# Gated linear attention in a hybrid trunk: keeping the 32x32 diagonal blocks of the scores in a compact array and multiplying them into the output block by block

## The chip, the cores and the metric

The kernel runs on one core of one Trainium2 chip. The metric is the device time of one execution in microseconds (us). The kernel before takes 1256.16 us, the median of 3 runs (1253.02 to 1259.6).

## What is computed

The reference is one layer of a trunk in which one input projection feeds four head groups (RetNet retention, gated DeltaNet, an S5 state space and GLA, gated linear attention); their gated outputs are concatenated and projected back. The change lies in the GLA group: 4 heads, keys 32 wide, values 64 wide, 2048 positions.

```python
def _gla(q, k, v, gk):                      # 4 heads, dk = 32, dv = 64
    cum = cumsum(gk within a chunk)
    rel = where(causal, cum_i - cum_j, -inf)
    scores[i, j] = sum_d q[i, d] * k[j, d] * exp(rel[i, j, d])
    o_intra = scores @ v                    # within the chunk
    state   = state * exp(cum_last) + (k * exp(cum_last - cum)).T @ v
    o_inter = (q * exp(cum)) @ state_before # from earlier chunks
    return o_intra + o_inter

y_gla = head_rmsnorm(o) * silu(gate)
out   = x + rmsnorm(concat(y_ret, y_dn, y_s5, y_gla) @ w_out)
```

## The kernel before, in words

All stages run on the one core, one after another, with neighbours overlapping: retention together with the S5 input projection, then GLA (`phase_gla`, L1198) with the S5 scan woven in as `side` steps, then DeltaNet (`phase_dn`), then the output projection (`phase_out`).

`phase_gla` works on 16 tiles of 128 positions, and a tile is treated as one chunk. For tile i the loop at L1387 issues `decays(i + 1)` (cumulative gate, its differences, exponentials; tile `gE`), `scores(i, 0)` for heads 0 and 1, the first half of the dense projections of later tiles (f16 products at L301 and L309 into `pa`), `output(i - 1)`, `mid(i)` (which loads and rescales the weights of DeltaNet after tiles 8, 9, 11 and 12; the rescaling on VectorE is L265), `scores(i, 1)` for heads 2 and 3, and the second half of the dense work. The S5 steps (lines 869 to 992; tiles `s5U`, `s5T`, `s5st`, `z`) run between the dense products. Small steps are put off with `later` and `string`, which release a chain of operations a few dense products apart, and with `due`, which issues what a buffer's next user needs. All operations so recorded carry line L153, so they are told apart by their tiles. The framework sets the final order of each engine's instructions from priorities and a timing model of its own; each engine then works through its list in order.

The scores of a tile are transposed (keys on partitions, queries along the row) and come in two kinds. The parts off the diagonal 32x32 blocks come out of PSUM straight into `gsT` ([128, 4, 128], one per tile parity) by three ScalarE copies (`copies`, L1337 to L1339). The diagonal 32x32 blocks are made of six levels, each a 32x32 product per block (L1299, 48 for two heads); `fin` (L1318) masks and adds them on VectorE for two heads at a time: one masked product `gpm` (128x384), one addition `gs` of 128x192 (tag `gs1`), one of 128x64 (tag `gs2`), and then four additions of 32x64, one for each 32-partition strip, that write the block to its place on the diagonal of `gsT` (L1330 to L1332). So `fin` is 7 VectorE operations for two heads, 14 a tile.

`output(i)` (L1347) takes the bank `o` (one buffer), multiplies the carried state (`gSbd`, L1351), adds the four heads' `gsT` times `gv` (L1353: 128x128 by 128x64 in f32), transposes `kl` (L1357), and later updates the state (L1363, L1367). `finish` squares, normalises and gates the result (`fsq`, `fss`, `fry`, `frt`, `frr`).

Elsewhere in the kernel small f32 products share a bank as the new ones do: in `dn_back` of DeltaNet (L1778 and L1779) the products alternate between the two 64-partition halves, and both halves of `pu` lie in one PSUM bank, as do both of `pw`.

Of the kernel before, what the change touches and what calls it, by code (L numbers as in the profile page):

```python
# [11 lines left out]
ALU = mybir.AluOpType  # L12
# [143 lines left out]
class Trunk:  # L156
# [1041 lines left out]
    def phase_gla(self, last, then, mid, side):  # L1198
        nc, A, NT = self.nc, self.A, self.NT
        NU = NT // 2  # L1200
        wqk, dqk = self.W["gqk"]
        P = self.pool("gla", bufs=2, side="right")
# [6 lines left out]
        nc.gpsimd.memset(Sbd, 0.0)  # L1209
        St = [S, Sbd]  # L1210
        blk = self.c("glablk")
        q2, k2, gk2, v, g, qk, q7, kl, el, done = ({} for _ in range(10))

        def stream(out, ops, fin):

# [75 lines left out]
        def scores(i, hp):  # L1291
            tk = slice((i % 2) * 128, (i % 2) * 128 + 128)
            q, k = q2[i // 2][:, tk], k2[i // 2][:, tk]
            sT = sT2[i % 2]
            box = []

            def mm(e, po, pn, c0, lh, rh, col):
                r = slice(32 * (2 * hp + e), 32 * (2 * hp + e) + 32)
                nc.tensor.matmul(box[0][po:po + pn, e, c0:c0 + rh.shape[1]], lh[r], rh[r], start=True, stop=True, tile_position=(32 * (2 * hp + e), col))  # L1299

            def first():
                self.due(lambda r, at: r == "gE")
                box.extend((self.ps("sc2"), self.count["sc2"]))

            yield first
            for e in range(2):
                yield lambda e=e: mm(e, 0, 64, 192, qk[i][:, 0, 0:64], qk[i][:, 0, 64:128], 0)
            for o, c0 in ((64, 64), (96, 0)):
                for e in range(2):
                    yield lambda e=e, o=o, c0=c0: mm(e, o, 32, 192, qk[i][:, 1, c0:c0 + 32], qk[i][:, 1, c0 + 32:c0 + 64], o)  # L1310
            for lv in range(6):
                for B in range(4):
                    cb = slice(32 * B, 32 * B + 32)
                    lh, rh = (qk[i][:, 2 + lv, cb], qk[i][:, 2 + lv, cb]) if lv < 5 else (k[:, cb], q[:, cb])
                    for e in range(2):
                        yield lambda e=e, B=B, lv=lv, lh=lh, rh=rh: mm(e, 32 * B, 32, lv * 32, lh, rh, 32 * B)

            def fin():  # L1318
                sc = box[0]
                ops = []  # L1320
                V = Later(nc.vector, ops)
                pm = self.t(P, [128, 2, 6, 32], "gpm")
                V.tensor_tensor(pm.rearrange("p e l i -> p e (l i)"), sc[:, :, 0:192],
                                msk.unsqueeze(1).to_broadcast([128, 2, 192]), op=ALU.mult)
                s1 = self.t(P, [128, 2, 3, 32], "gs1")
                V.tensor_tensor(s1, pm[:, :, 0:3, :], pm[:, :, 3:6, :], op=ALU.add)
                s2 = self.t(P, [128, 2, 32], "gs2")
                V.tensor_tensor(s2, s1[:, :, 0, :], s1[:, :, 1, :], op=ALU.add)
                sv = sT[:, 2 * hp:2 * hp + 2, :]
                for B in range(4):  # L1330
                    cb = slice(32 * B, 32 * B + 32)
                    V.tensor_tensor(sv[cb, :, cb], s2[cb], s1[cb, :, 2, :], op=ALU.add)  # L1332
                self.string(0, 3, ops, "sc2", box[1])

            def copies():
                sc, sv = box[0], sT[:, 2 * hp:2 * hp + 2, :]
                nc.scalar.activation(sv[0:64, :, 64:128], sc[0:64, :, 192:256], AF.Copy)  # L1337
                nc.scalar.activation(sv[64:96, :, 96:128], sc[64:96, :, 192:224], AF.Copy)
                nc.scalar.activation(sv[0:32, :, 32:64], sc[96:128, :, 192:224], AF.Copy)  # L1339

            def parts():
                done[i] = box[1]
                self.later(2, copies, "sc2", box[1])
                self.later(6, fin, "sc2", box[1])
            yield parts

        def output(i):  # L1347
            self.due(lambda r, at: r == "sc2" and at <= done[i])
            bank = self.ps("o")
            po, pk, pS = bank[:, 0:256], bank[:, 256:384], bank[:, 384:448]  # L1350
            nc.tensor.matmul(po, q7[i], St[1].rearrange("p h d -> p (h d)"), start=True, stop=False)  # L1351
            for h in range(4):
                nc.tensor.matmul(po[:, h * 64:(h + 1) * 64], sT2[i % 2][:, h, :], v[i][:, h, :], start=False, stop=(h == 3))  # L1353
            at = self.count["o"]
            if i + 1 < NT:
                kT = self.t(P, [128, 128], "gkT")
                nc.tensor.transpose(pk, kl[i], self.c("ident"))  # L1357
                nc.scalar.activation(kT, pk, AF.Copy)

                def update():  # L1360
                    for h in range(4):
                        r = slice(32 * h, 32 * h + 32)
                        nc.tensor.matmul(pS[r], kT[:, r], v[i][:, h, :], start=True, stop=True, tile_position=(0, 32 * h))  # L1363

                def state():
                    S = self.t(P, [128, 64], "gS")
                    nc.vector.scalar_tensor_tensor(S, St[0], el[i], pS, op0=ALU.mult, op1=ALU.add)  # L1367
                    Sbd = self.t(P, [128, 4, 64], "gSbd")
                    nc.gpsimd.tensor_tensor(Sbd, S.unsqueeze(1).to_broadcast([128, 4, 64]), blk.unsqueeze(2).to_broadcast([128, 4, 64]), op=ALU.mult)
                    St[:] = [S, Sbd]  # L1370

                self.later(10, update, "o", at)
                self.later(18, state, "o", at)
            self.finish(P, po, lambda: g[i], self.half(self.W["gg"][1], 4.0), 3, i)
# [5 lines left out]
        sT2 = [self.t(P1, [128, 4, 128], f"gsT{i}") for i in range(2)]  # L1380
# [6 lines left out]
        for i in range(NT):  # L1387
            self.due(lambda r, at: r == "gE")
            if i + 1 < NT:
                decays(i + 1)  # L1390
            dense = [v_ops(i + 1)] if i + 1 < NT else []
            dense += [g_ops(i)]
            u, part = (i + 3) // 2, (i + 1) % 2
            if u < NU:
                dense.insert(2 - part, qk_ops(u, part))
            dense = list(chain(*dense))
            h = len(dense) // 2

            for op in scores(i, 0):
                op()  # L1400
            self.emit(dense[:h], [side] * 2)
            if i > 0:
                output(i - 1)
            mid(i)
            for op in scores(i, 1):
                op()
            self.emit(dense[h:], [side])
        output(NT - 1)
        self.gP1, self.gP = P1, P

# [563 lines left out]
```

## Time and profile before

| what | value |
|---|---|
| median of 3 runs | 1256.16 us (1253.02 to 1259.6) |
| the profiled execution | 1256.04 us |
| span of its trace | 1253.8 us |
| mean granted TensorE clock | 0.937 of full speed |
| TensorE busy | 1129.3 us (90%) |
| VectorE busy | 960.0 us (77%) |
| ScalarE busy | 481.5 us (38%) |
| GpSimd busy | 459.8 us (37%) |

The profiled execution lies 0.1 us under the median of the runs, and 2.2 us of it lie outside the span. The shares are means over the whole kernel. The stage of the change is the loop over tiles in `phase_gla`; its first score product starts 327 us into the span and its last output product ends at 601 us, so the questions to ask of the trace are which engine is busy there, and what TensorE waits for there. In the rows PE is TensorE, DVE is VectorE, ACT is ScalarE and POOL is GpSimd.

### The profile page before, as it was taken

The numbers are of one execution on the slowest core, as the hardware profiler recorded it, in microseconds if no ns is written. First come the engines' busy times: TensorE is split into PE (matmuls) and PEld (weight loads), VectorE is DVE, ScalarE is ACT, GpSimd is POOL, SyncE is SP. The second block draws the span as 40 slices with busy tenths as digits, with TensorE's granted clock in tenths as the row PEclk, the third lists the DMA queues.
The fourth block names the chain that finished last, engine by engine and source line by source line (L and its number), as shares of the span: only waits on it lengthen the run. The fifth ranks groups of instructions, "written<-read, shape, count | busy, mean of one in ns | idle before, by whom it ended". The sixth has DMA issues, their size and how long they took to land. (4 is left out here: it accounts for less than half of the span.)

```text
span 1253.8 us, 37473 instructions
## 1 busy us (share of the span) xinstructions
PE 1129.3 (90%) x15175; PEld 933.1 (74%) x15175; DVE 960.0 (77%) x3429; ACT 481.5 (38%) x1076; POOL 459.8 (37%) x848
## 2 busy tenths in 40 slices
PE   4889999999899998988789989898899999899997
PEld 2767888888787777766667667676777777788886
DVE  7779655346899999998787676887888745778786
ACT  6623322126344444452433223342343453434332
POOL 3112121102755555552533423433423213434342
PEclk8899999999899999888989779898999989999999
DMA  8565611101211112121212112112112625566653
GB/s 291 142 159 137 166 64 68 35 22 60 62 30 35 35 35 55 35 55 22 86 45 33 27 21 38 26 51 39 29 50 44 157 80 149 180 182 177 190 132 104
DMA packets 186908, 104.91 MB, mean 84 GB/s; under 512 B 158000, under 2 KB 173552, under 8 KB 184560
## 3 DMA queue, kind: packets, MB, share of 16 engines
q1 hardware_dynamic: 186160, 102.00, 31.5%
q8 instruction: 119, 1.95, 0.6%
q10 hardware_dynamic: 576, 0.52, 0.1%
q14 instruction: 53, 0.43, 0.1%
HBM read 59.43 MB, written 26.23 MB: 68 GB/s over the span
## 5 line engine op out<-in xcount | busy, mean ns | idle before, releaser
L301 PEld LDWEIGHTS <-xT 128*128 128x128 f16 x3456 | 340.2, 101 | 82.4 <-issue 21.5
L301 PE MATMUL pa<-w,xT 128*128 128x256 f16 x3072 | 390.2, 283 | 6.7 <-DVE w L265 3.3
L309 PE MATMUL pa<-xT,w 128*128 128x256 f16 x1536 | 213.6, 290 | 14.4 <-ACT raw L1465 11.2
L309 PEld LDWEIGHTS <-w 128*128 128x128 f16 x1536 | 151.5, 103 | 44.1 <-issue 15.5
L1850 PE MATMUL o<-w,yT 128*128 128x256 f16 x1344 | 153.9, 275 | 6.7 <-DMA yT<-y 6.4
L1850 PEld LDWEIGHTS <-yT 128*128 128x128 f16 x1344 | 131.5, 98 | 26.6 <-DMA yT<-y 9.3
L153 DVE SCALAR_TENSOR_TENSOR cva<-raw,cw,cva 128x256 f32<-128x256 f32 x144 | 79.5, 554 | 1.4
L1861 POOL TENSOR_TENSOR ot<-of,npost 128x256 f32<-128x256 f32 x64 | 56.7, 904 | 47.4 <-ACT of L1859 47.2
L153 ACT ACTIVATE gE<-gE 128x384 f32<-128x384 f32 x96 | 43.8, 513 | 76.7 <-DVE gE L153 34.3
L265 DVE SCALAR_TENSOR_TENSOR w<-stg,wgs,w 128x256 f16<-128x256 f32 x96 | 52.4, 602 | 10.9 <-POOL w L262 10.0
L301 PE MATMUL pa<-wsu,xT 128*128 128x280 f16 x384 | 52.9, 298 | 8.2 <-DVE rgg L375 3.6
L1464 POOL COPY raw<-raw 128x3 f32<-128x3 f32 x48 | 14.8, 315 | 108.6 <-DVE cva L153 54.8
L1147 POOL TENSOR_TENSOR ropq<-ropm,ropn 128x256 f32<-128x256 f32 x16 | 12.8, 797 | 110.3 <-DVE ropn L1144 102.4
L371 ACT ACTIVATE th<-pa,hd 128x256 f32<-128x256 f32 x64 | 30.1, 470 | 53.8 <-PE pa L301 51.7
L408 ACT ACTIVATE fsq<-o 128x256 f32<-128x256 f32 x48 | 18.2, 379 | 82.1 <-PE o L1195 56.3
L153 DVE TENSOR_TENSOR gsT<-gs,gs 32x64 f32<-32x64 f32 x128 | 46.0, 360 | 1.9
L1860 DVE SCALAR_TENSOR_TENSOR ojk<-of 128x256 f32<-128x256 f32 x64 | 40.2, 629 | 9.4 <-ACT of L1859 6.8
L1285 POOL TENSOR_TENSOR gE<-gE,gk 128x64 f32<-128x64 f32 x112 | 34.3, 337 | 30.2 <-ACT gE L153 21.8
L1796 POOL TENSOR_TENSOR dKG<-dkh,dkgd 64x256 f32<-64x256 f32 x32 | 23.1, 721 | 57.8 <-PE c L1810 50.3
L153 DVE TENSOR_REDUCE fss<-fsq 128x4 f32<-128x256 f32 x48 | 19.8, 413 | 30.7 <-ACT fsq L408 30.6
L1476 ACT ACTIVATE cvt<-cva 128x256 f32<-128x256 f32 x48 | 19.9, 415 | 60.6 <-DVE cva L153 32.5
L1299 PE MATMUL sc<-gE 32*32 32x32 f32 (+1 forms) x2944 | 40.3, 203 | 2.5 <-DVE KK L910 2.5
(418 smaller groups left out, 2313.0 us busy)
## 6 DMA issues: line engine op xcount, KB each, us to landing
x<-in_x SPq DMA_DIRECT2D x16, 512.0 KB, 4.5
stg<-in_wi SPq DMA_DIRECT2D x8, 1024.0 KB, 4.8
yo<-y_d SPq DMA_DIRECT2D x14, 512.0 KB, 4.6
xo<-in_x SPq DMA_DIRECT2D x14, 512.0 KB, 3.6
out<-xo SPq DMA_DIRECT2D x13, 512.0 KB, 3.7
y_d<-fsq SPq DMA_DIRECT2D x48, 128.0 KB, 1.9
xT<-in_wi SPq DMA_DIRECT2D x4, 1024.0 KB, 7.0
rope<-in_rope SPq DMA_DIRECT2D x16, 256.0 KB, 3.2
```

Source lines behind the costliest of these rows:

```text
L153: return lambda *a, **k: self.ops.append(lambda: getattr(self.engine, name)(*a, **k))
L265: nc.vector.scalar_tensor_tensor(dst[:, 1, k, :], st[:, k, :], gs[:, k:k + 1], dst[:, 0, k, :], op0=ALU.mult, op1=ALU.subtract)
L301: yield lambda k=k, i=i, a=a, b=b: self.nc.tensor.matmul(out, xt[:, a, k, t0:t0 + 128], w[:, b, k, :], start=(k == 0 and i == 0), stop=(k ...
L309: yield lambda k=k, i=i, a=a, b=b: self.nc.tensor.matmul(out, w[:, b, k, c0:c0 + 128], xt[:, a, k, :], start=(k == 0 and i == 0), stop=(k ...
L371: nc.scalar.activation(th, ps[0], AF.Tanh, scale=self.half(dsc))
L1285: eng.tensor_tensor(x, x, src.rearrange("p (n w) -> p n w", w=2 * b)[:, :, a:a + b], op=ALU.mult)
L1299: nc.tensor.matmul(box[0][po:po + pn, e, c0:c0 + rh.shape[1]], lh[r], rh[r], start=True, stop=True, tile_position=(32 * (2 * hp + e), col))
L1476: nc.scalar.activation(th[0], a, AF.Tanh, scale=0.5)
L1796: nc.gpsimd.tensor_tensor(KG[r, c], f["kh"][r, t], f["kgd"][r, t, :].unsqueeze(2).to_broadcast([64, 4, 64]), op=ALU.mult)
L1850: nc.tensor.matmul(o, yT[:, a, k, :], w[:, b, k, :], start=(k == 0 and q == 0 and j % per == 0), stop=(k == 7 and q == 2 and j % per == pe ...
L1860: nc.vector.scalar_tensor_tensor(jk, of[:, cs], 1.0, of[:, cs], op0=ALU.mult, op1=ALU.mult, accum_out=so[:, j:j + 1])
L1861: nc.gpsimd.tensor_tensor(t1[:, cs], of[:, cs], npost[:, cs], op=ALU.mult)
```

## The change

`gpm`, `gs1` and `gs2` now hold all four heads of a tile. For heads 0 and 1 `fin` does only the masked product, into the first half of `gpm`. For heads 2 and 3 it does the masked product into the second half and then three additions for all four heads: 128x384 into `gs1`, 128x128 into `gs2`, and 128x128 in place in `gs2`. `fin` is 5 VectorE operations a tile, where it was 14. The diagonal blocks are no longer written to `gsT`, where they stay at the zeros of the start. `output` adds 16 products of 32x32 by 32x64 in f32, one for each head and each 32-partition strip, which take `gs2` straight and add to the same bank `o`.

```diff
@@ scores / fin @@
-                pm = self.t(P, [128, 2, 6, 32], "gpm")
-                V.tensor_tensor(pm.rearrange("p e l i -> p e (l i)"), sc[:, :, 0:192],
+                if hp == 0:
+                    pms[i] = self.t(P, [128, 4, 6, 32], "gpm")
+                pm = pms[i]
+                V.tensor_tensor(pm[:, 2 * hp:2 * hp + 2].rearrange("p e l i -> p e (l i)"), sc[:, :, 0:192],
                                 msk.unsqueeze(1).to_broadcast([128, 2, 192]), op=ALU.mult)
-                s1 = self.t(P, [128, 2, 3, 32], "gs1")
-                V.tensor_tensor(s1, pm[:, :, 0:3, :], pm[:, :, 3:6, :], op=ALU.add)
-                s2 = self.t(P, [128, 2, 32], "gs2")
-                V.tensor_tensor(s2, s1[:, :, 0, :], s1[:, :, 1, :], op=ALU.add)
-                sv = sT[:, 2 * hp:2 * hp + 2, :]
-                for B in range(4):
-                    cb = slice(32 * B, 32 * B + 32)
-                    V.tensor_tensor(sv[cb, :, cb], s2[cb], s1[cb, :, 2, :], op=ALU.add)
+                if hp == 1:
+                    pms.pop(i)
+                    s1 = self.t(P, [128, 4, 3, 32], "gs1", bufs=1)
+                    V.tensor_tensor(s1, pm[:, :, 0:3, :], pm[:, :, 3:6, :], op=ALU.add)
+                    s2 = self.t(P, [128, 4, 32], "gs2")
+                    sD[i] = s2
+                    V.tensor_tensor(s2, s1[:, :, 0, :], s1[:, :, 1, :], op=ALU.add)
+                    V.tensor_tensor(s2, s2, s1[:, :, 2, :], op=ALU.add)
                 self.string(0, 3, ops, "sc2", box[1])
@@ output @@
             for h in range(4):
-                nc.tensor.matmul(po[:, h * 64:(h + 1) * 64], sT2[i % 2][:, h, :], v[i][:, h, :], start=False, stop=(h == 3))
+                nc.tensor.matmul(po[:, h * 64:(h + 1) * 64], sT2[i % 2][:, h, :], v[i][:, h, :], start=False, stop=False)
+            D = sD.pop(i)
+            for h in range(4):
+                for o in range(0, 128, 32):
+                    r = slice(o, o + 32)
+                    nc.tensor.matmul(po[r, h * 64:(h + 1) * 64], D[r, h, :], v[i][r, h, :], start=False, stop=(h == 3), tile_position=(o, o))
```

## Rows read from the trace of the kernel before

**Rows 1.** stretches of the GLA loop: length, engines' busy time, clock, DMA

```profile
core 0: us, PE busy (x) PEld busy (x) DVE busy (x) ACT busy (x) POOL busy (x), PEclk, DMA share, GB/s
327.00:347.00 20.00, 16.03 (x378) 12.84 (x378) 18.50 (x40) 10.55 (x27) 19.25 (x41) 0.83 0.36 90
347.00:485.00 138.00, 128.96 (x2844) 108.44 (x2833) 132.87 (x442) 57.97 (x167) 79.63 (x197) 0.99 0.18 34
485.00:561.00 76.00, 67.49 (x1362) 54.51 (x1349) 71.38 (x242) 36.83 (x97) 44.83 (x100) 0.87 0.20 53
561.00:601.00 40.00, 34.15 (x665) 27.03 (x664) 31.90 (x122) 10.46 (x30) 11.18 (x27) 0.87 0.09 21
```

**Rows 2.** waits, 327 to 601 us, engine PE: total us, times, longest

```profile
PE z L932 <- ACT s5UT L920: 8.6, 5, 2.7
PE sc L909 <- DVE gpm L153: 4.0, 1, 4.0
PE o L1351 <- DVE fsq L153: 3.8, 3, 1.9
PE sc L982 <- DVE gpm L153: 3.2, 1, 3.2
```

**Rows 3.** groups by line, DVE, 327 to 601 us: busy us, mean ns, idle

```profile
L153 DVE TENSOR_TENSOR gsT<-gs,gs 32x64 f32<-32x64 f32 x128 | 46.0, 360 | 1.9
...
L153 DVE TENSOR_TENSOR gpm<-sc,glamask 128x384 f32<-128x384 f32 x32 | 17.4, 545 | 1.3 <-ACT gsT L1339 1.3
L153 DVE TENSOR_TENSOR gE<-gE 128x128 f32<-128x128 f32 x56 | 15.9, 291 | 0.0
...
L153 DVE TENSOR_TENSOR gs<-gpm 128x192 f32<-128x192 f32 x32 | 14.9, 466 | 0.5
...
L153 DVE TENSOR_TENSOR gs<-gs 128x64 f32<-128x64 f32 x32 | 8.9, 279 | 0.5
```

**Rows 4.** order of time (start us, length us), DVE, ACT, PE [idle before]

```profile
408.32 2.49 DVE L153 TENSOR_TENSOR gsT<-gs,gs 32x64 f32<-32x64 f32 x4
...
410.95 0.28 DVE L153 TENSOR_TENSOR gE<-gE 128x128 f32<-128x128 f32 x1
...
411.32 1.35 ACT L153 ACTIVATE gE<-gE 128x384 f32<-128x384 f32 x3 [2.31 <-DVE gE L153]
...
413.67 0.60 ACT L920 ACTIVATE s5UT<-z 128x512 f32<-128x512 f32 x1
...
414.32 1.08 PE L932 MATMUL z<-s5UT,s5PT 128*64 128x256 f32 x8 [2.66 <-ACT s5UT L920]
```

**Rows 5.** order of time, 541 to 549 us, DVE, then PE

```profile
541.33 5.32 DVE L265 SCALAR_TENSOR_TENSOR w<-stg,wgs,w 128x256 f16<-128x256 f32 x8 [0.47 <-POOL w L262]
...
546.89 1.57 PE L1299 MATMUL sc<-gE 32*64 32x64 f32 x88 [2.53 <-DVE KK L910]
```

**Rows 6.** order of time, PE: a tile's output, state update, next output

```profile
400.11 1.00 PE L1353 MATMUL o<-gv,gsT 128*128 128x64 f32 x8
...
404.29 0.32 PE L1363 MATMUL o<-gv,gkT 128*32 128x64 f32 x8
404.54 0.39 PE L309 MATMUL pa<-xT,w 128*128 128x256 f16 x2
...
417.63 1.00 PE L1353 MATMUL o<-gv,gsT 128*128 128x64 f32 x8
```

**Rows 7.** order of time, PE, 689 us: first and last of 58 instructions

```profile
689.11 0.22 PE L1779 MATMUL l<-dT,dkg 64*64 64x64 f32 x1
689.12 0.22 PE L1778 MATMUL l<-dv,dT 64*64 64x64 f32 x1
...
689.17 0.22 PE L1779 MATMUL l<-dT,dkg 64*64 64x64 f32 x1
...
689.94 0.22 PE L1779 MATMUL l<-dT,dkg 64*64 64x64 f32 x1
```

More of the change, by code (lines that the diff above doesn't have):

```diff
@@ L1211, in phase_gla @@
         blk = self.c("glablk")
-        q2, k2, gk2, v, g, qk, q7, kl, el, done = ({} for _ in range(10))
+        q2, k2, gk2, v, g, qk, q7, kl, el, done, pms, sD = ({} for _ in range(12))
         def stream(out, ops, fin):
```

## The prediction, made before the changed kernel ran

> **What bounds the kernel now.** I read the trace from the stage inwards: first the busy times of the GLA loop by stretch, then the waits of TensorE in it, then VectorE's groups by cost, then the order of time around single waits. The loop lasts 274 us, from 327 to 601, for 16 tiles: 17.1 us a tile. Adding up the four stretches, VectorE is busy 18.50 + 132.87 + 71.38 + 31.90 = 254.65 us (93%) and TensorE 246.63 us (90%) [rows 1]. Neither is at its full rate all the time: TensorE is idle 3.97, 9.04, 8.51 and 5.85 us in the four stretches, 27.4 us in all, and its granted clock is 0.83, 0.99, 0.87 and 0.87 there, which costs 0.17 x 20 + 0.01 x 138 + 0.13 x 76 + 0.13 x 40 = 19.9 us of full-speed work [rows 1]. So about 47 of the 274 us are not TensorE work at full speed, and some 227 us are. The reader should see that two engines are close to full at once: relieving VectorE can give back at most those 47 us, and whatever is added to TensorE is paid from them.
>
> Who makes TensorE wait? The longest sums are 8.6 us for `s5UT` from ScalarE, 4.0 and 3.2 us for the masked product `gpm` on VectorE, and 3.8 us for `fsq` on VectorE [rows 2]. The ScalarE wait is VectorE's too, as one case shows in order of time: the four strip additions hold VectorE for 2.49 us from 408.32; the difference `gE` queued behind them starts at 410.95; ScalarE's `gE`, which had idled 2.31 us for it, starts at 411.32; `s5UT`, next in ScalarE's list, starts at 413.67; and TensorE, idle 2.66 us, goes on at 414.32 [rows 4]. The very operations that the change removes stand at the head of that chain.
>
> **The change part by part.**
>
> **VectorE.** Removed are 128 strip additions (46.0 us), 32 additions of 128x192 (14.9) and 32 of 128x64 (8.9), together 69.8 us or 4.36 us a tile; the two masked products a tile stay [rows 3]. Added a tile are one addition of 128x384 and two of 128x128. The trace has no addition of 128x384 in this place: the masked product of that size takes 545 ns, and two of 128x192 would take 2 x 466 = 932 ns [rows 3]; I take 650, nearer to the row of the same size. For 128x128 the row is 291 ns [rows 3]; the second, in place and dependent on the first, I put at 330 (bounds 280 to 360, the last being the strip's own mean). Sum: 0.65 + 0.29 + 0.33 = 1.27 us a tile (bounds 1.11 to 1.65). Saved: 3.09 us a tile (2.7 to 3.25), 49 us in the loop. VectorE then has 254.65 - 49 = 205 us of work, and is no longer what fills the loop.
>
> **TensorE.** Added are 16 products a tile. The four products of L1353 stand in the trace as 8 instructions [rows 6], two for each product in f32, so the new ones are 32 instructions a tile; nothing is removed, since L1353 still multiplies whole 128x128 blocks. The nearest rows are small f32 products of the same 64 columns that fill different parts of the array: 58 instructions start between 689.11 and 689.94, 57 steps of 14.6 ns [rows 7]. Their blocks are 64x64 where the new ones are 32x32, but they too go four at a time to separate parts. That gives 32 x 14.6 = 0.47 us. Going to another block shape and back is not free: the 8 instructions of L1363 hold TensorE from 404.29 to 404.54, 0.25 us [rows 6], against 8 x 14.6 = 0.12, so I add 0.13. Together 0.60 us a tile, 9.6 us in the loop. Lower bound 0.47 (7.5 us); upper bound at L1363's own rate, 32 x 0.25 / 8 = 1.0 us (16 us).
>
> In the rows at 689 us, L1778 and L1779 start within 10 to 20 ns of one another though each lasts 220 ns, and both halves of `pu` lie in one bank [rows 7]: products from different rows of the array overlap while they write the same bank. The Trainium skill, page "TensorEngine Tiling (Array Packing)", section "Restrictions and Gotchas", says the opposite: "Different row tiles cannot access same PSUM bank simultaneously". The new products are just that, four row groups into the one bank `o`. By that sentence they would go singly, and the loop would lose instead of gain (the second rival has its price from rows); by the rows they overlap, and I go by the rows.
>
> **Waits.** `output` now waits for `gs2` where it waited for the strips in `gsT`. If `gs2` were late, the transpose of `kl` and the score products of the next half, queued behind it on TensorE, would be late, and ScalarE's copies after them. But the strips of the tile that is put out at 417.63 were done at 408.32 + 2.49 = 410.81 [rows 4, 6], 6.8 us early, and the new chain is shorter: 1.27 us behind the second masked product, where it was 0.47 + 0.28 + 4 x 0.36 = 2.19 [rows 3]. So I cost this wait at nothing; what hides it is the dense work between the second half's scores and the next output. If that cover were gone, it would cost up to 1.3 us a tile. The memory for four heads, ScalarE's copies to `gsT` and all DMA are as before; cost nothing.
>
> **What the relief gives back.** I take the four stretches of [rows 1] apart, idle time and clock together.
> - 327 to 347: 4.0 + 3.4 = 7.4 us. The wait is 4.0 us for the first `gpm` [rows 2], on which the first strip additions themselves depend. I expect 0 back.
> - 347 to 485: 9.0 + 1.4 = 10.4 us. These are the waits of the shape of [rows 4]. In that one the strips' 2.49 us become one addition of 0.33, 2.16 us sooner for a wait of 2.66, and the sums of the first half are gone from the list altogether. 80%: 8.3.
> - 485 to 561: 8.5 + 9.9 = 18.4 us. Here eight rescalings of weights hold VectorE 5.32 us in one piece, and TensorE's 2.53 us of idleness stands right behind it [rows 5]. The block stays; it only starts earlier. 40%: 7.4.
> - 561 to 601: 5.9 + 5.2 = 11.1 us: waits such as those for `fsq` [rows 2], which I read as the backlog of the stretch before. 85%: 9.4.
>
> Back: 25.1 us (bounds 10 and 40: only the steady stretch, or everything but the first). The clock's part is not independent: it is lowest in the stretches with the longest waits [rows 1], and I let it return in the same share.
>
> **The sum.** 1256.0 (the profiled execution; the median of the runs is 1256.2, no difference that counts) - 25.1 + 9.6 = 1240.5 us. What is late next is TensorE itself: 227 + 9.6 = 237 us of work in a loop of about 258, with VectorE at 205.
>
> **The rivals.**
>
> *The waits stay (no change).* VectorE's list is in fixed order and ScalarE's `gE` still stands ahead of `s5UT`. If the order, not the load, makes the waits, or if GpSimd (155 us of the loop by the sum of its four stretches [rows 1]) takes VectorE's place in the `gE` chain, only some 10 us come back and the new products take 9.6: 1256. For it: the longest stretch of losses (18.4 us) hangs on the rescaling block, which is not touched. Against it: the removed strips are the very hold-up in [rows 4].
>
> *The new products go one at a time (slower).* Place: `output` on TensorE. Price: 32 instructions at L1353's 1.00 / 8 = 0.125 us [rows 6], 4.0 us a tile, 64 us in all: 1256 - 25 + 64 = 1295. It decides from 25.1 / 16 = 1.6 us a tile, 49 ns an instruction; up to there the change still breaks even. Against it: the steps of 14.6 ns in [rows 7]; for it only that four row groups, not two, write one bank here.
>
> *Everything but the first stretch comes back (faster still).* 40 us back, 9.6 paid: 1226. For it: the clock falls only where TensorE waits [rows 1], so losses could vanish together. Against it: the rescaling block.
>
> **How the numbers follow.** Forecast as worked out, between 1231 and 1250: 0.53. The waits stay, 1250 to 1262: 0.25. Products singly or another order that loses, over 1262: 0.11. Everything back, under 1231: 0.11. The range from 1229 to 1261 leaves out most of the last two, about 2 in 10. A difference of 0.5% (6.3 us) is about what a measurement of this kernel can tell from none. Faster by more than that, under 1249.9: the forecast's cases but a few and those that are faster still, 0.63. Within it: 0.24. Slower: 0.13.
>
> **What would show each step right or wrong.** VectorE's groups in the loop: the strips gone, one 128x384 and two 128x128 additions at 0.65 and 0.3 us, VectorE's busy time in the loop near 205 us. TensorE's new group at the output line: 32 instructions in about 0.6 us between L1353 and the transpose; singly they would take 4. The waits: `s5UT` nearly gone from TensorE's list, those behind the rescaling still there. The clock in the last three stretches closer to 1. The forecast is wrong if TensorE starts to wait for `gs2`, if the waits move to GpSimd's `gE`, or if the new products stretch out.

## The result and the profile after

The changed kernel takes 1239.24 us (median of 4 runs, 1231.29 to 1240.62) beside 1257.88 us for the kernel before (median of 4). The ratio is 0.987, 95% interval 0.9824 to 0.9915: 1.3% faster, some 16 us. In two further sets of runs, beside the experiments, it gave 0.9845 (0.9814 to 0.9877) and 0.9865 (0.9833 to 0.9897). The forecast was 1240.5 us.

The profiled execution has a span of 1236.9 us, against 1253.8. Its loop over tiles in GLA, from the first score product to the last product into `o`, lasts from 328.6 to 590.5 us: 261.9 us, where it was 273.9 in the trace of before. So 12.0 of the 16.9 us between the two spans lie in the loop. DeltaNet behind it is 7.7 us shorter, and the stages ahead of the loop and at the end are together 2.8 us longer. Loop and DeltaNet are both taken up below.

The changed kernel, busy time by stretch; the stretches are cut at the same places of the work as in [rows 1], and the columns are those of [rows 1]:

```profile
328.60:348.00 19.40, 15.44 (x362) 12.53 (x362) 17.70 (x35) 10.64 (x27) 19.27 (x41) 0.82 0.39 93
348.00:482.50 134.50, 133.30 (x3067) 112.22 (x3055) 109.94 (x364) 59.84 (x166) 85.82 (x197) 1.00 0.18 35
482.50:554.50 72.00, 65.09 (x1546) 54.31 (x1545) 61.25 (x202) 36.68 (x96) 46.65 (x101) 0.95 0.22 56
554.50:590.50 36.00, 32.08 (x761) 26.24 (x760) 27.57 (x100) 11.13 (x33) 12.50 (x39) 1.00 0.15 30
sum 261.90, PE 245.90 PEld 205.29 DVE 216.47 ACT 118.29 POOL 164.24; mean PE 61.48 PEld 51.32 DVE 54.12 ACT 29.57 POOL 41.06
```

In the second stretch TensorE is busy 133.3 of 134.5 us at full clock, where [rows 1] had 129.0 of 138. VectorE has gone from 254.65 to 216.47 us. The first stretch is nearly as it was (19.4 us, where it was 20); the third still has idle time (6.9 us) and a clock of 0.95.

The changed kernel, who waited for whom, TensorE in the loop (total us, times, longest):

```profile
PE sc L909 <- DVE gpm L153: 4.0, 1, 4.0
PE sc L982 <- DVE gpm L153: 3.0, 1, 3.0
PE o L1354 <- DVE fsq L153: 2.7, 2, 1.4
PE z L932 <- ACT s5UT L920: 2.3, 2, 1.9
PE sc L1299 <- DVE KK L910: 1.5, 1, 1.5
PE sc L982 <- DVE gs L153: 0.8, 4, 0.2
```

The wait for `s5UT`, at 8.6 us the longest of [rows 2], is down to 2.3. The two waits for `gpm` stand where they stood. TensorE's new products are in no row as waiting.

The changed kernel, VectorE's groups in the loop (count, busy us, mean ns):

```profile
L153 DVE TENSOR_TENSOR gs<-gpm 128x384 f32<-128x384 f32 x16 | 11.5, 718 | 0.0
L153 DVE TENSOR_TENSOR gs<-gs,gs 128x128 f32<-128x128 f32 x16 | 8.7, 547 | 0.0
L153 DVE TENSOR_TENSOR gs<-gs 128x128 f32<-128x128 f32 x16 | 5.5, 346 | 0.0
```

These 25.7 us take the place of the 69.8 us of [rows 3]. The three groups of strips and halves are gone.

The changed kernel, TensorE in order of time around one output (start us, length us):

```profile
402.14 1.00 PE L1356 MATMUL o<-gv,gsT 128*128 128x64 f32 x8
403.07 0.65 PE L1361 MATMUL o<-gv,gs 32*32 32x64 f32 x32
403.65 0.33 PE L1365 MATMUL o<-cst,gkl 128*128 128x128 f32 x1
403.91 0.50 PE L1299 MATMUL sc<-gE 32*64 32x64 f32 x9
```

The 32 new instructions start from 403.07 on, and the transpose behind them starts at 403.65. The first and the last of the 32 start 0.43 to 0.44 us apart in all 16 tiles. From the first L1356 to the transpose it is 1.51 us, in this tile as in the 14 others that have a transpose; in the trace of before it was 0.83, from 400.11 [rows 6] to this row of the same view:

```profile
400.94 0.28 PE L1357 MATMUL o<-cst,gkl 128*128 128x128 f32 x1
```

So the products cost 0.68 us a tile, of which 0.25 are the change of shape on either side. The 14 ns from one of the 32 starts to the next are a mean: in the trace's records the starts come in fours, 7 ns apart, and from one four to the next it is about 56 ns. Two rows of the changed kernel's view of the tile `gs` (duration in ns, least, median and most) are used further down:

```profile
L1361 PE MATMUL o<-gv,gs x512: 214/214/238, 355.4 to 590.3; 32*32 32x64 f32 x171
...
L153 DVE TENSOR_TENSOR gs<-gs,gs x16: 278/492/725, 344.4 to 586.0; 128x128 f32<-128x128 f32 x16
```

### The profile page after: what moved, and what is told of

The parts are those of the page before. It is cut to its first block, busy times and chain, and to the rows that moved or that the text cites. A ratio compares the mean times of both kernels' runs of the same rounds, so it can differ in the third digit from the quotient of the medians.

```text
span 1236.9 us, 38345 instructions
## 1 busy us (share of the span) xinstructions
PE 1125.1 (91%) x15687; PEld 933.9 (76%) x15687; DVE 924.1 (75%) x3285; ACT 484.2 (39%) x1076; POOL 471.0 (38%) x848
## 5 line engine op out<-in xcount | busy, mean ns | idle before, releaser
L301 PEld LDWEIGHTS <-xT 128*128 128x128 f16 x3456 | 335.3, 100 | 78.8 <-issue 24.4
L301 PE MATMUL pa<-w,xT 128*128 128x256 f16 x3072 | 382.0, 278 | 6.8 <-DVE w L265 3.1
L153 DVE TENSOR_REDUCE fss<-fsq 128x4 f32<-128x256 f32 x48 | 19.9, 414 | 52.8 <-ACT fsq L408 52.8
L1868 DVE SCALAR_TENSOR_TENSOR ojk<-of 128x256 f32<-128x256 f32 x64 | 40.2, 629 | 10.5 <-ACT of L1867 7.9
L1179 POOL TENSOR_TENSOR sg<-sbd,cst 64x128 f32<-64x128 f32 x30 | 12.8, 425 | 82.8 <-DVE sbd L1180 71.2
L1299 PEld LDWEIGHTS sc<-gE 32*32 32x32 f32 (+1 forms) x2944 | 33.7, 105 | 8.8 <-DVE KK L910 1.7
```

Of the source, the lines that this page charges most:

```text
L153: return lambda *a, **k: self.ops.append(lambda: getattr(self.engine, name)(*a, **k))
L301: yield lambda k=k, i=i, a=a, b=b: self.nc.tensor.matmul(out, xt[:, a, k, t0:t0 + 128], w[:, b, k, :], start=(k == 0 and i == 0), stop=(k ...
L1868: nc.vector.scalar_tensor_tensor(jk, of[:, cs], 1.0, of[:, cs], op0=ALU.mult, op1=ALU.mult, accum_out=so[:, j:j + 1])
```

## The experiments

The theory to be tested: VectorE's load makes TensorE wait and lets its clock fall, the change takes that load away, and TensorE pays for the new products. The rivals are those of the prediction, and, once the profiles were compared, one more: that part of the gain belongs to DeltaNet. The length of the GLA loop in each profile is set beside the ratio of each kernel, since what lies behind the loop varies from one execution to the next. Each loop is read from one profiled execution; where a kernel was profiled more than once, its loops are 273.9 and 273.0 us (before) and 261.9, 265.5 and 262.0 us (changed). In the three sets of runs of the experiments the kernel before took 1250.6 to 1252.2 us, so ratios are compared, not times.

**The products alone.**

```diff
--- the kernel before
+            D = zD
+            for h in range(4):
+                for o in range(0, 128, 32):
+                    r = slice(o, o + 32)
+                    nc.tensor.matmul(po[r, h * 64:(h + 1) * 64], D[r, h, :], v[i][r, h, :], start=False, stop=(h == 3), tile_position=(o, o))
...
+        zD = self.t(P1, [128, 4, 32], "gzD")
+        nc.gpsimd.memset(zD, 0.0)
```

> The kernel before with the 16 products of 32x32 a tile added to it, on a block of zeros, so that the result is the same and VectorE keeps all its strip additions. Theory (the products are paid in full by a TensorE that has little slack): 0.67 us a tile as in the profile of the changed kernel, up to 10.7 us more than before, 1262 to 1269. Rival (TensorE waits for VectorE anyway in this loop, and the products fit into its waits): within 4 us of before, 1256 to 1260.

Measured: ratio 0.9961 (0.9933 to 0.999), 1244.97 us beside 1250.58. Nothing was paid, and the theory's 10.7 us fell for this kernel; the rival was right. The loop of the kernel with the products alone, and then of the kernel before in a second profiled execution (columns as in [rows 1]):

```profile
329.40:602.30 272.90, 250.31 (x5703) 208.14 (x5704) 247.73 (x841) 117.40 (x319) 159.94 (x376) 0.96 0.19 43
```

```profile
328.20:601.20 273.00, 242.82 (x5197) 201.08 (x5197) 254.61 (x841) 115.75 (x319) 154.82 (x364) 0.94 0.19 41
601.20:1069.40 468.20, 425.17 (x5967) 337.33 (x5966) 360.72 (x1202) 177.61 (x401) 168.66 (x279) 0.91 0.27 65
```

The two loops are equally long. With the products TensorE is busy 7.5 us longer and has the better clock (0.96 against 0.94). As long as VectorE sets the length of the loop, added work on TensorE takes up time that was idle or lost to the clock. (The second row of the second fence is the stage behind the loop, used below.)

**The relief alone.**

```diff
--- the changed kernel
-            D = sD.pop(i)
-            for h in range(4):
-                for o in range(0, 128, 32): ...
+            sD.pop(i)
```

> The changed kernel without the 16 products a tile; the diagonal blocks are summed as in the change but are left out of the output. Theory (the gain is VectorE's relief, and the products cost TensorE 0.67 us a tile): some 25 us faster than before, 10 us faster than the changed kernel, 1226 to 1232. Rival (what is left to wait for sets the loop, and the products fill those waits): the same as the changed kernel, 1236 to 1241.

Measured: ratio 0.9828 (0.9783 to 0.9873), 1226.71 us. Its loop:

```profile
326.90:578.20 251.30, 234.79 (x5196) 196.22 (x5196) 219.07 (x697) 117.58 (x319) 161.92 (x364) 0.97 0.20 45
```

251.3 us: 22.6 less than before, and 10.6 less than the changed kernel. So once VectorE is relieved the same products are paid in full, 0.66 us a tile. For the loop the theory holds, and with the run above it says when: the price of TensorE's work depends on which engine sets the loop. The time of the whole kernel shows less of it. By the ratios this kernel is 2 to 5 us faster than the changed one, not 10, and the intervals overlap; so the 10.6 us rest on the loops.

**The products on one part of the array after another.**

```diff
--- the changed kernel
-            for h in range(4):
-                for o in range(0, 128, 32):
+            for o in range(0, 128, 32):
+                for h in range(4):
```

> The changed kernel with the two loops of the new products exchanged: the four heads of one 32-partition strip follow one another, so that four products in a row use the same part of the array. Theory (the products are cheap because neighbours go to different parts): the block of 32 instructions takes at least 1.5 us, where it is 0.43 to 0.44, so 16 to 30 us more, 1255 to 1270. Rival (they are cheap because each is small, some 14 ns of issue apiece): the same block length, 1236 to 1242.

Measured: ratio 1.0039 (1.0007 to 1.0071), 1254.48 us: the whole gain is gone. The loop, then the block of products in order of time:

```profile
331.10:610.10 279.00, 265.84 (x5703) 221.07 (x5704) 214.66 (x697) 118.91 (x319) 159.78 (x376) 0.94 0.19 42
```

```profile
406.61 1.39 PE L1361 MATMUL o<-gv,gs 32*32 32x64 f32 x32
407.93 0.33 PE L1365 MATMUL o<-cst,gkl 128*128 128x128 f32 x1
```

The transpose follows the block's start by 1.32 us where it was 0.58. The block's starts spread over 1.18 us, 38 ns an instruction in the mean instead of 14. I had expected 1.5 at least, so the size was too high, but the direction is clear: the loop is 17 us longer (14 against the longest loop of the changed kernel), of which 16 x 0.74 = 11.8 are the block; the rest goes with a lower clock (0.94 against 0.97). The order of the two loops decides whether this change gains at all.

**The merged sums with strips on VectorE, no products.**

```diff
--- the changed kernel, products taken out
-                    V.tensor_tensor(s2, s2, s1[:, :, 2, :], op=ALU.add)
+                    for B in range(4):
+                        cb = slice(32 * B, 32 * B + 32)
+                        V.tensor_tensor(sT[cb, :, cb], s2[cb], s1[cb, :, 2, :], op=ALU.add)
```

> The sums once a tile for four heads as in the change, but then four additions of 32x128 that put the blocks into their places, and no new products. VectorE has 9 operations a tile where before had 14 and the change 5. Theory (VectorE's load makes the waits, and TensorE pays for the products): VectorE saves some 1.7 us a tile of the 3.1, so about half to two thirds of the 25 us come back and nothing is paid, 1238 to 1246, close to the changed kernel. Rival (it is the strips in themselves that hold up the chain): hardly faster than before, 1250 to 1258.

Measured: ratio 0.9871 (0.9824 to 0.9919), 1233.96 us, like the changed kernel. The loop, then its longest wait of TensorE:

```profile
327.90:591.50 263.60, 237.01 (x5201) 197.89 (x5201) 234.84 (x745) 116.86 (x319) 158.99 (x364) 0.96 0.19 43
```

```profile
PE z L932 <- ACT s5UT L920: 11.8, 7, 3.7
```

This loop is as long as the changed one by another road: TensorE has no products to pay, but idles 26.6 us, and the wait for `s5UT` is back. Summing once for four heads and multiplying block by block are two separable halves of the change, and the first by itself is worth about as much as both: the second, for which the change is named, added nothing here that could be measured.

**The strips copied by ScalarE, no products.**

```diff
--- the changed kernel, products taken out
                     V.tensor_tensor(s2, s2, s1[:, :, 2, :], op=ALU.add)
+                    C = Later(nc.scalar, ops)
+                    for B in range(4):
+                        cb = slice(32 * B, 32 * B + 32)
+                        C.activation(sT[cb, :, cb], s2[cb], AF.Copy)
```

> The change's three additions for four heads, but ScalarE copies the four strips (32x128 each) from the compact array into their places, and there are no new products. Theory (once VectorE is relieved TensorE sets the loop, and the products cost it 0.67 us a tile): the loop is as long as without the products, 251 to 255 us, 20 to 25 us faster than before. Rival (ScalarE works in order, and the copies, which wait for VectorE's sums, hold up the exponentials and the copy of s5UT behind them): loop 258 to 266 us, 6 to 15 us faster than before.

Measured: ratio 0.984 (0.9805 to 0.9875), 1232.35 us. In the same set the changed kernel had 1231.47 us, so the two cannot be told apart. The loop, then the new group on ScalarE:

```profile
326.90:584.60 257.70, 240.87 (x5196) 200.49 (x5196) 218.57 (x697) 135.38 (x383) 161.32 (x364) 0.94 0.20 44
```

```profile
L153 ACT ACTIVATE gsT<-gs 32x128 f32<-32x128 f32 x64 | 19.6, 307 | 31.4 <-DVE gs L153 30.6
```

The loop of 257.7 us lies between the two expectations. TensorE pays nothing, but its clock is 0.94, and ScalarE idles 30.6 us in front of the copies until VectorE's sums are there.

**The rescaling of weights spread out.**

```diff
--- the changed kernel, prep_b
-        for k in range(8): ... (issued at once)
+        for k in range(8): ... (recorded with Later on the three engines)
+        if spread: (6 for the two loads inside the loop)
+            self.string(2, spread, ops, "wb")
...
```

> The changed kernel, with the 16 steps that rescale DeltaNet's weights inside the loop (tiles 9 and 12) released six dense products apart where they were issued in one piece. Theory (what is left of the waits and of the clock's loss between tiles 9 and 13 comes from that block on VectorE): the waits for gpm at about 492 us and for the first scores at about 542 us vanish, the loop is 255 to 259 us, 3 to 7 us faster than the changed kernel. Rival (VectorE is late there for its load as a whole): the waits move, the loop stays at 260 to 264 us.

Measured: ratio 0.9885 (0.9856 to 0.9915), 1237.27 us. The loop, then its waits of TensorE:

```profile
329.40:594.10 264.70, 247.78 (x5703) 206.63 (x5703) 214.17 (x697) 118.05 (x319) 163.48 (x376) 0.96 0.20 44
```

```profile
PE z L939 <- ACT s5UT L927: 4.8, 3, 3.5
PE sc L916 <- DVE gpm L153: 4.0, 1, 4.0
PE o L1361 <- DVE fsq L153: 3.3, 2, 2.0
PE sc L989 <- DVE gpm L153: 2.5, 1, 2.5
```

The theory fell. The waits at 492 and 542 us did vanish, but others came in their place (for `s5UT` and, 70 us later, for `gpm`), and the loop is no shorter. That is what the rival expected: VectorE is late in those tiles for its load as a whole. No run tests that reading further.

**The part behind the loop.** In the profiles the DeltaNet stage, up to the first product of the output stage, was 476.4 us before and 468.7 after, with no line of it changed. The framework orders each engine's instructions by a timing model, and after the change 425 of VectorE's 1202 instructions of this stage stand in other places in the trace, and TensorE's order differs too. (The kernel with the products alone, and the one with the loops exchanged, have the changed kernel's order there.) To ask what that order is worth, 16 products on zeros in the last two tiles alone give the kernel before, or the kernel with ScalarE's strips, exactly the changed kernel's order on these two engines; and taking the products of the last two tiles away gives the changed kernel the order of before, but for a few instructions.

```diff
--- the kernel before; the same on the kernel with ScalarE's strips
+            if i >= NT - 2:
+                (the 16 products on zD)
```

> The kernel before with 16 products on a block of zeros in the last two tiles alone. The GLA loop has 1.3 us more for TensorE; but behind it the instructions of DeltaNet come in the order that they have in the changed kernel, which is not the order of the kernel before. Theory (some 5 us of the gain come from that order in DeltaNet, not from the change): 3 to 6 us faster than before, loop 272 to 276 us. Rival (the order is worth nothing, and what the profiles show in DeltaNet is chance): within 2 us of before.

Measured: ratio 1.0002 (0.9973 to 1.0031), 1252.17 us, as the rival expected.

> The kernel in which ScalarE copies the four strips, with the same products on zeros in the last two tiles, which give DeltaNet the order of the changed kernel. Theory (relief and order add up): the 20 us of that kernel, 4 to 5 more for the order, less 1.3 for the products, so 22 to 25 us faster than before, which is faster than the changed kernel. Rival (the order is worth nothing): 17 to 20 us.

Measured: ratio 0.9873 (0.9831 to 0.9916), 1232.56 us beside 1252.23, loop 259.2 us: 19.7 us faster by the medians and 15.9 by the ratio, again nearer to the rival.

```diff
--- the changed kernel
+            if i < NT - 2:
                 (the 16 products on D)
```

> The changed kernel without its products in the last two tiles, where the diagonal blocks are left out of the output; DeltaNet then has the order of the kernel before, but for a few instructions. Theory (relief alone): loop 258 to 264 us, 10 to 14 us faster than before, and so 3 to 6 us slower than the changed kernel beside it. Rival (the order is worth nothing): as fast as the changed kernel or 1 us faster.

Measured: ratio 0.9922 (0.9889 to 0.9956), 1240.35 us beside 1252.23. Here the theory was nearer: 12 us faster than before, and 8 slower than the changed kernel.

> The changed kernel again, on the chip of the three kernels beside it: loop 260 to 266 us, 14 to 20 us faster than before.

Measured: ratio 0.9865 (0.9833 to 0.9897), 1232.42 us, loop 262.0 us.

> The changed kernel once more, on the same chip as the two kernels beside it, for its stage lengths: loop 260 to 264 us, and 12 to 20 us faster than before in all.

Measured: ratio 0.9845 (0.9814 to 0.9877), 1231.47 us.

> The kernel before once more, for the length of its DeltaNet stage, which was 476 us in its first profile and 468 us in the changed kernel's. If the 8 us are chance of one execution, it is 466 to 472 here; if they belong to the order of that kernel's instructions, 474 to 479. The GLA loop: 272 to 276 us.

Measured: 1248.0 us, loop 273.0 us, DeltaNet 468.2 us (the fence further up): 8 us shorter than in the first profile of the same kernel, so by the expectation those 8 us were chance of one execution.

The stage behind the loop in four profiles, one fence each: the kernel before with the products in the last two tiles; the changed kernel without them; the changed kernel's second and third execution (its loop is the first row of each):

```profile
328.60:603.20 274.60, 247.06 (x5255) 203.42 (x5256) 254.62 (x841) 115.76 (x319) 155.68 (x376) 0.92 0.19 42
603.20:1081.00 477.80, 431.76 (x5973) 342.51 (x5973) 358.35 (x1202) 177.47 (x401) 170.08 (x267) 0.89 0.26 63
```

```profile
325.30:588.70 263.40, 247.71 (x5644) 206.01 (x5644) 216.47 (x697) 118.30 (x319) 162.91 (x364) 0.96 0.19 43
588.70:1061.20 472.50, 422.67 (x5969) 336.88 (x5966) 357.81 (x1202) 177.98 (x401) 169.79 (x279) 0.91 0.27 65
```

```profile
328.20:593.70 265.50, 248.45 (x5703) 206.69 (x5703) 216.87 (x697) 118.34 (x319) 164.10 (x376) 0.96 0.20 44
593.70:1054.00 460.30, 411.46 (x5974) 329.94 (x5973) 360.81 (x1202) 177.99 (x401) 170.55 (x267) 0.94 0.28 66
```

```profile
329.60:591.60 262.00, 245.88 (x5703) 205.23 (x5703) 216.65 (x697) 118.28 (x319) 164.10 (x376) 0.97 0.20 44
591.60:1056.50 464.90, 420.54 (x5973) 335.28 (x5974) 358.38 (x1202) 177.78 (x401) 170.15 (x267) 0.92 0.27 65
```

These runs do not agree on what the order is worth. Two say nothing: the kernel before with the changed kernel's order is not faster, its DeltaNet stage is 477.8 us, and the kernel with ScalarE's strips gained nothing by it. Two say 5 to 8 us: the changed kernel with the order of before is 0.6% slower than the changed kernel in the same set of runs (the intervals just touch), at loops of 263.4 and 262.0 us, and the kernel with the products alone was 0.4% faster than before at an equal loop. No one of the causes tried fits all four. The stage's length over the profiles does not decide it either: with the changed kernel's order on both engines it is 460.3 to 468.7 us in six profiles and 477.8 in the seventh, and with the order of before, or that but for a few instructions, 468.2 to 476.4 us in five. What the rows do show is that the stage's length goes with the granted clock in it, 460.3 us at 0.94 and 477.8 at 0.89, and that one and the same kernel differs by 8 us between two executions. The loop is shorter in every profile of the changed kernel, by 7.5 to 12.0 us; what the part behind the loop contributes stays open.

## Why the prediction was right, and where it was not

**The bound.** The prediction took 47 us of the loop for idle time and lost clock and 227 us for work. The same split (length, less idle time, less the clock's loss from the rows; the clock is rounded to 0.01, so each loss is good to 1.4 us) over the loops of before, the changed kernel and five of the experiments:

| loop | length | TensorE idle | clock's loss | work |
|---|---|---|---|---|
| before (sum of the stretches of [rows 1]) | 274 | 27.4 | 19.9 | 227 |
| products alone | 272.9 | 22.6 | 10.9 | 239 |
| changed | 261.9 | 16.0 | 7.1 | 239 |
| relief alone | 251.3 | 16.5 | 7.5 | 227 |
| products on the same part | 279.0 | 13.2 | 16.7 | 249 |
| merged strips on VectorE | 263.6 | 26.6 | 10.5 | 226 |
| strips on ScalarE | 257.7 | 16.8 | 15.5 | 225 |

The work comes out at 225 to 227 us wherever there are no products, at 239 with them as the change has them, and at 249 with the loops exchanged. The bound was read rightly: what the relief gave back came out of idle time and clock, and the work stayed.

**The relief.** Forecast: 25.1 us given back. Measured: idle time and clock fell from 47.3 to 23.1 us, that is 24.2 given back, and 22.6 by the loop of the kernel with the relief alone. By stretch the forecast was 0, 8.3, 7.4 and 9.4 us given back; idle time and clock's loss fell by 0, 9.2, 7.9 and 7.2. The first three were sized about right. The last was mis-sized: I had read its waits as the backlog of the rescaling and let 85% of its 11.1 us return, and 65% did. The waits that were to go (`s5UT`) went, and of those that were to stay the first `gpm` stayed whole (4.0 us) and the one behind the rescaling at 1.5 of 2.5 us.

**The products.** Forecast 0.60 us a tile, measured 0.68: 0.43 in steps of 14 ns in the mean, as in [rows 7], and 0.25 for the change of shape, where I had 0.13 from L1363. The runs add what the forecast did not say: the price is paid only because the relief makes TensorE the bound. In the kernel before it is nothing.

**VectorE.** This was the term most off. Forecast 1.27 us a tile for the three additions (0.65, 0.29, 0.33); measured 0.72 + 0.35 + 0.55 = 1.61, inside the bounds at their upper end. The in-place addition alone has 278 to 725 ns. The trace shows what the spread goes with. Of the 16 additions of 128x384, the four with no GpSimd tensor_tensor beside them took 547 to 559 ns, and the twelve with one beside them throughout 749 to 806. One of each, VectorE's row and then, for the longer one, GpSimd's at that time (start us, length us):

```profile
492.39 0.55 DVE L153 TENSOR_TENSOR gs<-gpm 128x384 f32<-128x384 f32 x1
408.01 0.80 DVE L153 TENSOR_TENSOR gs<-gpm 128x384 f32<-128x384 f32 x1
```

```profile
407.83 1.30 POOL L685 TENSOR_TENSOR s5P<-s5c,s5c 128x128 f32<-128x128 f32 x2
```

The masked product of the same size, which I took for the nearest row, takes 540 to 558 ns with or without GpSimd beside it; it reads `sc` out of PSUM. So it was the wrong neighbour, and the trace of before had a better one: its additions of 128x192 take 340 to 359 ns alone and 386 to 648 beside such an instruction. That GpSimd's work is the cause was not tested by a run.

VectorE ended at 216 us in the loop instead of 205. The three additions are 5.4 of these 11 us; most of the rest lies in operations that the change does not touch, such as `fry<-frt,fry` on 128x4, at 10.3 us where it had 6.9. What this cost the loop no run shows; with VectorE busy for 216 of 262 us I take it for little.

**The rivals.** "The waits stay" had the rescaling block for it, and that block's waits did stay, but not the steady ones. "One at a time" did not happen with the loops as they are written; with the loops exchanged, which sends neighbours to one part of the array, the steps are 38 ns in the mean and the gain is gone. The break-even of 49 ns that the prediction worked out left out the change of shape; with its 0.25 us a tile it is some 41. The Trainium skill's sentence on row tiles and PSUM banks (page "TensorEngine Tiling (Array Packing)", section "Restrictions and Gotchas") does not agree with the trace, as far as starts can tell: the 32 instructions go to four row groups and one bank, and four of them start within 21 ns, where on one row group the next starts only after some 56 ns.

**The sum.** Right to 1.3 us in the first measurement, but with luck in it. In the loop the forecast was 15.5 us; the profiles have 12.0 in the first pair (0.9 us less came back, the products cost 1.3 more, and the rest is within the rounding of the clock), and 10.4 by the means of two executions of before (273.5) and three of the changed kernel (263.1). The ratios give 16 to 19 us. The difference, 4 to 9 us, came from behind the loop, which the prediction left as it was, and its cause is open.

Of the other versions that compute the whole result none beats the changed kernel clearly: ScalarE's strips and the merged sums with strips on VectorE equal it.

## What to carry to other kernels

Where two engines are both nearly full, split the loop into work, idle time and lost clock before sizing a change: the first is what an addition to the bound engine adds to, the other two are all that a relief can give back. The price of an operation added to an engine is not a number of its own; the same 16 products a tile cost the loop nothing while VectorE set it and 10.6 us after. For the time of a VectorE operation take a row that reads from the same places and has the same neighbours at work, not only one of the same size: here 128x384 took 540 to 558 ns in one place and up to 806 in another. Test the halves of a change by themselves: here the merged sums alone gave as much as the whole. Small products on parts of the array should be ordered so that neighbours go to different parts (14 against 38 ns an instruction here). When a gain shows up in a stage whose code did not change, measure several executions before explaining it.

## What the runs showed of the hardware that was not expected

Small f32 products of 32x32 by 32x64 start every 14 ns in the mean when neighbours go to four different parts of the array, and every 38 ns when four in a row go to the same part (0.43 and 1.18 us for 32 instructions). The start records show what lies behind the means. As the change has them, four start 7 ns apart and the next four come about 56 ns after the four before; with the loops exchanged, the steps at the block's two ends, where one part has work alone, are 55 to 56 ns but for the first, of 80, and in between mostly 25 to 30. I read this as one instruction every 56 ns on each part in either order, and the order as deciding how many parts work at once.

Entering and leaving such a block among 128x128 products costs about 0.25 us, the same in both orders (from the first L1356 to the first of the block 0.93 us, where the transpose had come after 0.83; behind the last of the block 0.15).

VectorE's f32 additions of 128x384 took longer by a third to a half while GpSimd ran a tensor_tensor of its own (749 to 806 ns against 547 to 559), and the masked product of that size, which reads one operand out of PSUM, did not (540 to 558).

The clock's loss in a loop followed TensorE's waits less closely than I had assumed: the loops with 16 to 17 us of idle time have mean clocks from 0.94 to 0.97.
